# Half of one gate of an encoder block by seven products, in rows, with the sums of x kept on chip

## The chip, the cores and the metric

The kernel runs on one core of one Trainium2 chip, in one launch. The metric is the device time in microseconds (us). Five engines work side by side from queues of their own: TensorE (PE, matmuls; its weight loads are listed as PEld), VectorE (DVE), ScalarE (ACT), GpSimd (POOL) and SyncE (SP, which here only starts DMA transfers). SBUF is the working memory on the chip, with 128 partitions; PSUM holds the results of matmuls.

## The reference

One encoder block on x of 256 tokens by 2048 channels, in float32. What matters here is that eight pieces come out of one input projection, two branches are gated, and the result is merged:

```python
xn = rms_norm(x, norm_pre_w[l])
z = xn @ w_in[l]                       # 2048 x 13312
u_lru, g_lru, q, k, v, g_attn, m_lru, m_attn = jnp.split(z, split_at, axis=-1)
...
y_a = h.astype(x.dtype) * jax.nn.silu(g_lru)          # h: RG-LRU of the convolved u_lru, both directions
...
y_b = windowed_gqa(q, k, v, attn_sink[l]) * jax.nn.silu(g_attn)
merged = (jax.nn.sigmoid(m_lru) * (y_a @ w_proj_a[l])
          + jax.nn.sigmoid(m_attn) * (y_b @ w_proj_b[l]))
x = x + rms_norm(merged @ w_out[l], norm_post_w[l])
```

Each of g_lru, g_attn, m_lru and m_attn is 2048 columns wide. The change concerns the second 1024 columns of g_attn.

## The kernel before

**Numbers in two parts.** A product in float32 is made of products of a faster type, fp32r: each operand is split into a high part (a cast) and a low part (what the cast lost), and three products are added: high x high, high x low, low x high. A *half* of weights is a tile of 128 x 1024. ACT casts it to wh (`split`, L220), DVE subtracts to get wl (L222). The x parts, xs0 to xs7, are made once.

**Steps.** `load_plan` turns three written lists, START, MERGE and OUT, into steps; PE does them in that order. Each step uses 1 MB of weights, two halves. There are three kinds. A *blk* (letters g, h, w, k, q) is half of the sum for two column blocks of 128, so that "h8.0 h8.1" gives 256 columns of g_attn, with columns on partitions and the 256 tokens along the row (`add_pair`). A *quad* (u, v, p, b, o) is a quarter of 512 columns. A *part* (letters L, M, N, A, O: class `Seven`) belongs to a scheme that makes 1024 columns from seven products, m1 to m7, instead of eight, each of them in two parts (.0, .1); its results are in rows, tokens on partitions and columns along the row. The products need sums of blocks of x (`x_sums`) and sums of blocks of the weights. The weights' sums are built in *cells* of SBUF: a cell is loaded, and later blocks are added in flight by POOL's DMA (`accum_op`) or, for the pairs named in ADDED, by DVE (L225). The sums of x are made once, stored to DRAM as `away`, and loaded again for each part that needs them (`x_sum`, L357).

**What sets the order.** The program is written by the loop at the end of `body`, half by half. Transfers are issued 3 to 5 steps ahead (`fetch`), the cast four halves and the low part three halves ahead of PE (L1183 and on). Everything else is put at a tick of PE's order with `at` or `soon` (a part is one tick, other steps two): evacuations of PSUM, the chains of the RG-LRU (`lru_pair`, whose starts LRU shifts), attention heads (`heads`). Within an engine's queue the order is that of the program.

**Memory.** Most tiles of 4 KB a partition come from one pool of 45 *units* (`unit`); a new tile takes the place of the oldest one that is free, and waits for its last reader. PSUM has four single banks (`bank`) and two double ones (`banks`). Results that are needed much later are parked in DRAM: `park` stores a unit of 512 KB, `back` loads it.

**The gate that changes.** For "h", `silu_evac` copies the sums (ACT, L611), adds the low products (DVE, L604), scales by the row factor (DVE, L600), takes the sigmoid (ACT, L757) and multiplies (DVE, L758), then parks the unit `sga` when it has four blocks. For L, M, N and A, `gate_sum` combines the products (DVE, L784) and takes the sigmoid in rows (ACT, L792).

Of the kernel before, what the change touches and what calls it, by code (L numbers as in the profile page):

```python
# [21 lines left out]
P = 128  # L22
# [32 lines left out]


MERGE = """p0.0 p0.1 p0.2 p0.3 p1.0 p1.1 p1.2 p1.3 p2.0 p2.1 p2.2 Am1.0 p2.3 p3.0 p3.1 Am1.1 p3.2 Am5.0 p3.3
    b0.0 Am5.1 b0.1 Am3.0 b0.2 b0.3 Am3.1 b1.0 Am6.0 b1.1 b1.2 Am6.1 b1.3 Am7.0 b2.0 Am7.1 b2.1 Am2.0 b2.2 Am2.1 b2.3 Am4.0 b3.0
    Am4.1 Om1.0 b3.1 Om5.0 b3.2 b3.3""".split()
OUT = """o2.0 o2.1 Om1.1 o2.2 Om5.1 Om2.0 o2.3 Om3.0 Om6.0 Om3.1 o3.0 Om6.1 Om2.1 o3.1 Om7.0 Om7.1 Om4.0 Om4.1  # L60
    o3.2 o3.3""".split()

START = """u0.0 u0.1 u0.2 u0.3 v0.0 v0.1 v0.2 v0.3 g0.0 g0.1 h0.0 h0.1 w4.0 w4.1 g2.0 g2.1 h2.0 h2.1 w6.0 w6.1 g4.0 g4.1
    Lm1.0 h4.0 h4.1 Lm1.1 w8.0 Lm2.0 w8.1 Lm2.1 g6.0 Lm5.0 g6.1 h6.0 Lm5.1 h6.1 Lm3.0 w10.0 Lm3.1 w10.1 Lm6.0 g8.0
    Lm6.1 g8.1 h8.0 Lm7.0 h8.1 Lm7.1 w12.0 Lm4.0 w12.1 Lm4.1 g10.0 Mm1.0 g10.1 h10.0 Mm1.1 h10.1 Mm2.0 w14.0 Mm2.1
    w14.1 Mm5.0 g12.0 Mm5.1 g12.1 h12.0 Mm3.0 h12.1 Mm3.1 q0.0 Mm6.0 q0.1 Mm6.1 q0.2 q0.3 Mm7.0 g14.0 Mm7.1 g14.1
    Mm4.0 h14.0 Mm4.1 h14.1 Nm1.0 k0.0 k0.1 Nm1.1 k2.0 Nm2.0 k2.1 Nm2.1 q1.0 Nm5.0 q1.1 Nm5.1 q1.2 q1.3 Nm3.0 q2.0
    Nm3.1 q2.1 Nm6.0 q2.2 Nm6.1 q2.3 Nm7.0 q3.0 q3.1 Nm7.1 q3.2 Nm4.0 q3.3 Nm4.1""".split()
TURN = ((2, 6, 12, 15), (2, 6, 10, 13), (2, 6, 9, 11))
XSUM = (18, 22, 26, 30, 34, 38, 42, 46)  # L70
LRU = (-4, 0, 2, 2, 2, 2, 2, 4)
QUADS = {"u": ("w_in", U0), "v": ("w_in", V0), "p": ("w_proj_a", 0),
         "b": ("w_proj_b", 0), "o": ("w_out", 0)}
ADDED = {'A': {'m3': 'm6', 'm2': 'm4'}, 'O': {'m3': 'm6'}}
PAIRS = {"g": GL0, "h": GA0, "w": U0, "k": K0, "q": Q0}
SEVENS = {"L": ("w_in", ML0 + 1024), "M": ("w_in", ML0), "N": ("w_in", MA0), "A": ("w_in", MA0 + 1536), "O": ("w_out", 0)}


PV_CW = 0
# [37 lines left out]
def body(ctx, tc, x, x0, xT, wall, wlru, pvec, npost, ident_d, mask_d, rope_d, out):  # L117
# [9 lines left out]
    def unit(name, dt=F32, shape=(P, 4, S)):  # L127
        return units.tile(list(shape), dt, tag="u", name=name)
# [207 lines left out]
    def turned_sums_of(name, src, done):  # L336
# [9 lines left out]
        soon(lambda: parts_of(t[:, :, 0], t[:, :, 1], f))  # L346
        done(t)

    def x_sums(n):
        v = unit(f"xa{n}")  # L350
        nc.vector.tensor_tensor(v[:, 0:2], xs[n][:, :, 0].bitcast(F32), xs[n][:, :, 1].bitcast(F32), ALU.add)
        store = lambda t: nc.sync.dma_start(away[n // 4][:, :, n % 4], t.rearrange("p a b c -> p a (b c)").bitcast(F32))
        sums_of(f"xx{n}", v[:, 0:2], lambda t: soon(lambda: store(t), 7), v[:, 2:4])

    def x_sum(name, s, q):
        t = unit(name, F32R, (P, 4, 2, P))
# [3 lines left out]
    class Seven:  # L360
# [22 lines left out]
        def fetch(self, p, lead):  # L383
            m, q = p[2:]
            fresh = ("m1", "m3") if self.sums is None else ()
            if self.sums is None:
                if lead == 4 and m in fresh:
                    self.start(self.where(m), q)
                if lead == 4 and SEVEN[m][0][0] == "s":
                    self.kept[m, q] = x_sum(f"{self.name}{m}{q}", SEVEN[m][0], q)  # L390
            if lead == 5 and m in ("m5", "m6", "m7", "m4")[self.sums is not None:] and m not in ADDED.get(self.name, {}).values():
                load(self.cell(m, q), p, True)
# [356 lines left out]
    def silu_evac(units_list, n):  # L749
        def done(ps):  # L750
            if n % 4 == 0:
                units_list.append(unit(f"sg{n}"))
            dst = units_list[n // 4][:, n % 4:n % 4 + 2]

            def sigmoid():
                sg = half_unit(f"sig{n}", "p")
                nc.scalar.activation(sg, dst, AF.Sigmoid)  # L757
                soon(lambda: nc.vector.tensor_tensor(dst, dst, sg, ALU.mult))  # L758
# [27 lines left out]
    def gate_sum(gates, first=2, step=1):  # L786
# [177 lines left out]
    def heads(g, b, end):  # L964
        def start():
            h, l = unit(f"qh{g}", F32R), unit(f"ql{g}", F32R)
            parts_of(h, l, qs.pop(g))
            soon(lambda: back("sga", sga, g, (P, 4, S)), 6)
            for j in range(4):
                if j % 2 == 0:  # L970
                    both = {}
                head(4 * g + j, h, l, b + HEADS_AT[j], both, end)

        if g in QPARK:
            at(b - 8, lambda: back("q", qs, g, (P, 4, S)))
# [301 lines left out]
```

## Time and profile before

| | |
|---|---|
| median of 3 runs | 875.31 us (874.67 to 876.77) |
| profiled execution | 874.13 us |
| its span in the trace | 872.4 us |
| TensorE clock granted | 0.998 |
| PE, PEld busy | 99%, 85% |
| DVE, ACT, POOL busy | 84%, 74%, 7% |
| DMA | 248.96 MB, mean 285 GB/s |

In the rows of a profile, a group is "line engine operation out<-in shapes xcount | busy us, mean ns of one | idle time of the engine before them, and what ended it". A timeline row gives the start, the length and the work, with the idle time before it in brackets; neighbouring instructions of a group may overlap, so a price is taken from start to start. L12 is line 12 of the kernel. Tiles carry the names of the program: Lm1 is PSUM of product m1 of L, raw63 the weights of step 63, ga8 the PSUM of h8.

### The profile page before, as it was taken

The numbers are of one execution on the slowest core, as the hardware profiler recorded it, in microseconds if no ns is written. First come the engines' busy times: TensorE is split into PE (matmuls) and PEld (weight loads), VectorE is DVE, ScalarE is ACT, GpSimd is POOL, SyncE is SP. The second block draws the span as 40 slices with busy tenths as digits, with TensorE's granted clock in tenths as the row PEclk, the third lists the DMA queues.
The fourth block names the chain that finished last, engine by engine and source line by source line (L and its number), as shares of the span: only waits on it lengthen the run. The fifth ranks groups of instructions, "written<-read, shape, count | busy, mean of one in ns | idle before, by whom it ended". The sixth has DMA issues, their size and how long they took to land.

```text
span 872.4 us, 12283 instructions
## 1 busy us (share of the span) xinstructions
PE 862.8 (99%) x4450; PEld 739.7 (85%) x4450; DVE 736.4 (84%) x988; ACT 642.1 (74%) x923; POOL 62.5 (7%) x93
## 2 busy tenths in 40 slices
PE   9999999999999999999999999999999999999996
PEld 8888888888888888888888888888888888888885
DVE  6898999899797989789678688997669769999885
ACT  7689687878789696787776699976557455575654
POOL 0000001012000011100101100000000100000200
PEclk9999999999999999999999999999999999999999
DMA  8757599999959999996989996998999988988972
GB/s 322 288 195 231 204 358 250 351 335 285 330 212 270 311 296 319 300 324 219 299 326 305 301 323 204 311 315 329 301 293 365 305 302 244 327 296 319 257 196 97
DMA packets 66508, 248.96 MB, mean 285 GB/s; under 512 B 6416, under 2 KB 22544, under 8 KB 50960
## 3 DMA queue, kind: packets, MB, share of 16 engines
q1 hardware_dynamic: 52672, 208.86, 64.7%
q0 software_dynamic: 9792, 35.66, 21.1%
q10 hardware_dynamic: 3984, 3.67, 1.3%
q8 instruction: 35, 0.57, 0.3%
q14 instruction: 25, 0.20, 0.1%
HBM read 227.71 MB, written 20.45 MB: 284 GB/s over the span
## 4 chain that ended last, share of the span: by engine, by line
PE 88%; issue 4%; DVE 4%; DMA 2%; ACT 1%; SPq 0%; ACTq 0%; POOLq 0%; DVEq 0%
PE ga L256 7%; PE q L256 7%; PE gl L256 7%; PE u L256 5%; PE Mm L424 4%; PE Lm L424 4%; PE Nm L424 4%; PE ga L254 4%; PE gl L254 4%; PE q L254 4%; PE Om L424 3%; PE u L254 3%; PE pa__5770 L276 3%; PE pa__5514 L276 3%; PE o__7585 L276 3%
## 5 line engine op out<-in xcount | busy, mean ns | idle before, releaser
L222 DVE TENSOR_TENSOR wl<-raw,wh 128x1024 fp32r<-128x1024 f32 (+1 forms) x252 | 299.6, 1202 | 55.1 <-ACT wh L220 46.0
L220 ACT CAST wh<-raw 128x1024 fp32r<-128x1024 f32 (+1 forms) x251 | 253.8, 1035 | 67.2 <-DMA raw<-wall_dram 40.8
L256 PE MATMUL ga<-xs,wh 128*128 128x512 f32 x256 | 63.5, 391 | 0.0
L256 PE MATMUL gl<-xs,wh 128*128 128x512 f32 x256 | 63.4, 391 | 0.0
L256 PE MATMUL q<-xs,wh 128*128 128x512 f32 x256 | 63.2, 391 | 0.0
L256 PEld LDWEIGHTS gl<-xs,wh 128*128 128x128 f32 x256 | 47.0, 188 | 9.1
L256 PEld LDWEIGHTS q<-xs,wh 128*128 128x128 f32 x256 | 47.0, 188 | 9.0
L256 PEld LDWEIGHTS ga<-xs,wh 128*128 128x128 f32 x256 | 46.7, 188 | 8.8
L256 PE MATMUL u<-xs,wh 128*128 128x512 f32 x192 | 47.5, 391 | 0.0
L256 PEld LDWEIGHTS u<-xs,wh 128*128 128x128 f32 x192 | 35.2, 188 | 6.7
L254 PEld LDWEIGHTS q<-xs,wl 128*128 128x128 f32 x256 | 33.2, 191 | 1.2
L254 PEld LDWEIGHTS ga<-xs,wl 128*128 128x128 f32 x256 | 33.0, 191 | 1.2
L254 PE MATMUL q<-xs,wl 128*128 128x256 f32 x256 | 34.0, 283 | 0.0
L254 PEld LDWEIGHTS gl<-xs,wl 128*128 128x128 f32 x256 | 32.8, 191 | 1.2
L254 PE MATMUL ga<-xs,wl 128*128 128x256 f32 x256 | 33.5, 283 | 0.0
L254 PE MATMUL gl<-xs,wl 128*128 128x256 f32 x256 | 33.2, 283 | 0.0
L254 PEld LDWEIGHTS u<-xs,wl 128*128 128x128 f32 x192 | 24.6, 191 | 0.9
L254 PE MATMUL u<-xs,wl 128*128 128x256 f32 x192 | 24.9, 283 | 0.0
L673 DVE SCALAR_TENSOR_TENSOR uu<-upad,pv,uu 128x256 f32<-128x256 f32 x48 | 23.2, 483 | 1.7
L757 ACT ACTIVATE sig<-sg 128x512 f32<-128x512 f32 x16 | 10.2, 636 | 14.2 <-DVE sg L600 14.2
L896 DVE CUSTOM_DVE_ANT_0 p<-sc,table,pv 128x256 f32<-128x256 f32 x32 | 16.1, 540 | 5.1 <-PE sc L231 5.1
L902 ACT ACTIVATE p<-p,nm 128x256 f32<-128x256 f32 x32 | 16.0, 500 | 3.2 <-DVE nm L897 3.2
(519 smaller groups left out, 2085.6 us busy)
## 6 DMA issues: line engine op xcount, KB each, us to landing
raw<-wall_dram SPq DMA_DIRECT2D x121, 1024.0 KB, 7.7
lraw<-wlru_dram SPq DMA_DIRECT2D x8, 512.0 KB, 6.1
away<-xx SPq DMA_DIRECT2D x8, 512.0 KB, 8.7
Lm<-away SPq DMA_DIRECT2D x8, 512.0 KB, 12.6
Mm<-away SPq DMA_DIRECT2D x8, 512.0 KB, 13.8
Nm<-away SPq DMA_DIRECT2D x8, 512.0 KB, 14.6
turn<-pt SPq DMA_DIRECT2D x32, 128.0 KB, 5.0
pl<-turn SPq DMA_DIRECT2D x8, 512.0 KB, 7.2
```

Source lines behind the costliest of these rows:

```text
L220: cast(hs, raw)
L222: nc.vector.tensor_tensor(ls, raw, hs.bitcast(F32), ALU.subtract)
L254: nc.tensor.matmul(ps[:, 1], wl[:, sl], a[:, 0], start=False, stop=False)
L256: nc.tensor.matmul(ps, wh[:, sl], a, start=k == 0, stop=k == KT - 1)
L276: nc.tensor.matmul(got[t], a[:, i], (wl if low else wh)[:, sl], start=k + low + i == 0, stop=low == 1 and k == KT - 1)
L424: nc.tensor.matmul(self.ps[b], a[i], (wl if low else wh)[:, sl], start=fresh and j + low + i == 0, stop=last and j + low == 2, skip_group_ ...
L673: nc.vector.scalar_tensor_tensor(u, up[:, j, tap:tap + S], cw[:, tap:tap + 1], u, ALU.mult, ALU.add)
L757: nc.scalar.activation(sg, dst, AF.Sigmoid)
L896: nc.vector.tensor_tensor_reduce(p[:, t], sc[:, t], table["mask"][:, t], rtok_sc[:, t:t + 1], sk, ALU.add, ALU.max, m[:, t:t + 1])
L902: nc.scalar.activation(p[:, t], p[:, t], AF.Exp, bias=nm[:, t:t + 1], accum_out=dn[:, t:t + 1])
```

## The change

Eight steps, h8.0 to h14.1, go. A new Seven "H" gives the same 1024 columns in fourteen parts. Its results stand in rows, while the branch's attention output needs columns on partitions, so `silu_rows` does: combine (DVE), sigmoid with the tokens' scale (ACT, `hs`), scale and multiply (DVE), then a *turn*: four TensorE transposes into PSUM (`ht`), one copy by ACT into the same unit (`hr`), and a store of 256 KB by SP into `parksga`, so that four stores of 256 KB stand for two of 512 KB. A turn is put at the next start of the second step of a pair (`seconds`). The sums of x stay in SBUF from `x_sums` until M's m7; L, M and H read them there, and only N and A load them from `away`. N's m6 is built by DVE from m3's weights (ADDED) instead of by POOL. START is laid anew, mostly with two parts after a blk; in MERGE, Om1.0 and Om5.0 each move one step later; seven of the LRU's starts move to 0 or stay there; heads prepare one tick earlier.

```diff
-    b0.0 Am5.1 b0.1 Am3.0 b0.2 b0.3 Am3.1 b1.0 Am6.0 b1.1 b1.2 Am6.1 b1.3 Am7.0 b2.0 Am7.1 b2.1 Am2.0 b2.2 Am2.1 b2.3 Am4.0 b3.0
-    Am4.1 Om1.0 b3.1 Om5.0 b3.2 b3.3""".split()
+    b0.0 Am5.1 b0.1 Am3.0 b0.2 b0.3 Am3.1 b1.0 Am6.0 b1.1 b1.2 Am6.1 b1.3 Am7.0 b2.0 Am7.1 b2.1 Am2.0 b2.2 Am2.1 b2.3 Am4.0 b3.0 Am4.1 b3.1 Om1.0 b3.2 Om5.0 b3.3""".split()
...
-LRU = (-4, 0, 2, 2, 2, 2, 2, 4)
+LRU = (-4, 0, 0, 0, 0, 0, 0, 0)
...
-ADDED = {'A': {'m3': 'm6', 'm2': 'm4'}, 'O': {'m3': 'm6'}}
+ADDED = {'A': {'m3': 'm6', 'm2': 'm4'}, 'O': {'m3': 'm6'}, 'N': {'m3': 'm6'}}
...
-SEVENS = {"L": ("w_in", ML0 + 1024), "M": ("w_in", ML0), "N": ("w_in", MA0), "A": ("w_in", MA0 + 1536), "O": ("w_out", 0)}
+SEVENS = {"L": ("w_in", ML0 + 1024), "M": ("w_in", ML0), "N": ("w_in", MA0), "A": ("w_in", MA0 + 1536), "H": ("w_in", GA0 + 1024), "O": ("w_out", 0)}
...
+    seconds, hs, n = [], 0, 0
+    for p in plan:
+        if p[0] == "blk":
+            n += 1
+            if n % 2 == 0:
+                seconds.append(hs)
+        hs += 1 if p[0] == "part" else 2
...
-        sums_of(f"xx{n}", v[:, 0:2], lambda t: soon(lambda: store(t), 7), v[:, 2:4])
+        def done(t):
+            xsum[n] = t
+            soon(lambda: store(t), 7)
+
+        sums_of(f"xx{n}", v[:, 0:2], done, v[:, 2:4])
...
-                if lead == 4 and SEVEN[m][0][0] == "s":
+                if lead == 4 and SEVEN[m][0][0] == "s" and self.name in "NA":
...
+            elif self.name in "NA":
+                src = self.kept[m, q][:, j]
             elif self.sums is None:
-                src = self.kept[m, q][:, j]
+                src = xsum[n][:, SUMS.index(a)]
...
+                if self.name == "M":
+                    xsum.clear()
...
+    def silu_rows(g):
+
+        def done(t, c, ps, other, sign):
+            u = unit(f"hr{g}{c}{t}")
+            f, y = flat(u)[:, 0:512], u[:, 2:4].rearrange("p a (b s) -> p (a b) s", b=2)
+            rt = rtok[:, t:t + 1]
+
+            def sigmoid(src):
+                sg = flat(half_unit(f"hs{c}{t}", "p"))
+                nc.scalar.activation(sg, src, AF.Sigmoid, scale=rt)
+                soon(lambda: nc.vector.scalar_tensor_tensor(f, src, rt, sg, ALU.mult, ALU.mult))
+                at(min(b for b in seconds if b > now[0] + 2), turn)
+
+            def turn():
+                pt = banks(f"ht{c}{t}", (P, 4, P))
+                for j in range(4):
+                    nc.tensor.transpose(pt[:, j], f[:, j * P:(j + 1) * P], ident)
+                nc.scalar.copy(y, pt)
+                soon(store, 5)
+
+            def store():
+                key = "sga", g + c
+                if key not in parked:
+                    parked[key] = dram.tile([P, 1024], F32, name=f"parksga{g + c}")
+                nc.sync.dma_start(parked[key].rearrange("p (j s) -> p j s", j=4)[:, :, t * P:(t + 1) * P], y)
+
+            if other is None:
+                sigmoid(ps)
+            else:
+                combine(f, ps, other, sign)
+                soon(lambda: sigmoid(f))
+        return done
+
+    Seven("H", xs, None, silu_rows(2))
...
-        at(b - 2, start)
+        at(b - 3, start)
```

Three places of the order follow, each before and after. (In the changed kernel the lines of a helper stand some lower: the cast is L222, the low part L224.)

PE around the second pair of q0, in the middle of the first stage, before (q00 and q02 are the PSUM of q's two pairs, Mm1 that of a product of M, Mm61 the sums of x loaded for M's m6):

```order
L256 MATMUL q00_3579<-xs7_262,wh72_1_3603 128x512 x2
L424 MATMUL Mm1_2826<-wh73_0_3634,Mm61_3531 128x512 x4
L424 MATMUL Mm1_2826<-wl73_0_3635,Mm61_3531 128x512 x2
L424 MATMUL Mm1_2826<-wh73_1_3644,Mm61_3531 128x512 x4
L424 MATMUL Mm1_2826<-wl73_1_3645,Mm61_3531 128x512 x2
L256 MATMUL q02_3741<-xs0_123,wh74_0_3661 128x512 x2
L256 MATMUL q02_3741<-xs1_134,wh74_0_3661 128x512 x2
```

A part of M ends and the second pair of q0 begins. After, in the same pair, between its first and its second step:

```order
L435 MATMUL Mm1_3547<-wh74_1_3554,xs6_257 128x512 x2
L435 MATMUL Mm1_3547<-wh74_1_3554,xs7_262 128x512 x2
L435 MATMUL Mm1_3547<-wl74_1_3555,xs6_257 128x512
L435 MATMUL Mm1_3547<-wl74_1_3555,xs7_262 128x512
L831 MATMUL ht11_3645<-ident_92,hr211_3359 128x128 x4
L831 MATMUL ht01_3651<-ident_92,hr201_3540 128x128 x4
L258 MATMUL q02_3575<-xs0_123,wh75_0_3571 128x512 x2
```

M's part is now one of m1 and reads xs; behind it two turns, ht11 and ht01 (of the rows hr211 and hr201), stand next to each other.

ACT at the same place, before:

```order
L611 COPY q0f_3707<-q00_3579 128x512
L220 CAST wh75_0_3709<-raw75_3654 128x1024
L220 CAST wh75_1_3719<-raw75_3654 128x1024
L738 ACT_TABLE_LOAD
L738 ACTIVATE th12_3596<-th12_3596 128x1024
L436 COPY Mu_3735<-Mm1_2826 128x512
L220 CAST wh76_0_3737<-My0a_3251 128x1024
L853 COPY q0r_3758<-q0f_3707 32x256 x2
L220 CAST wh76_1_3763<-My0b_3252 128x1024
L792 ACT_TABLE_LOAD
L792 ACTIVATE mg1_3761<-mg1_3761,rtok_167 128x512
L220 CAST wh77_0_3786<-raw77_3729 128x1024
```

Casts of steps 75 to 77 with pieces of the LRU, of M and of q between them. After:

```order
L222 CAST wh75_0_3571<-raw75_3534 128x1024
L751 ACT_TABLE_LOAD
L751 ACTIVATE th12_3454<-th12_3454 128x1024
L222 CAST wh75_1_3597<-raw75_3534 128x1024
L222 CAST wh76_0_3623<-raw76_3564 128x1024
L222 CAST wh76_1_3633<-raw76_3564 128x1024
L832 COPY hr211_3359<-ht11_3645 128x512
L832 COPY hr201_3540<-ht01_3651 128x512
L447 COPY Mm1_3657<-Mm1_3547 128x512
L222 CAST wh77_0_3659<-raw77_3617 128x1024
```

The two copies of the turns stand behind the casts of steps 75 and 76, the second directly behind the first.

DVE around g12.0, which is step 63 in both orders, before (sg8_2583 is the unit of sga):

```order
L758 TENSOR_TENSOR sg8_2583<-sg8_2583,sig10_3119 128x512
L222 TENSOR_TENSOR wl61_1_3122<-raw61_3045,wh61_1_3121 128x1024
L222 TENSOR_TENSOR wl62_0_3151<-Mx0a_2663,wh62_0_3150 128x1024
L784 SCALAR_TENSOR_TENSOR mg0_3173<-Mm2_3068,Mm1_2995 128x512
L222 TENSOR_TENSOR wl62_1_3161<-Mx0b_2664,wh62_1_3160 128x1024
L222 TENSOR_TENSOR wl63_0_3176<-raw63_3141,wh63_0_3175 128x1024
L712 SCALAR_TENSOR_TENSOR th10_3114<-gr10_3019,th10_3114 128x1024
L222 TENSOR_TENSOR wl63_1_3202<-raw63_3141,wh63_1_3201 128x1024
L222 TENSOR_TENSOR wl64_0_3229<-Mx1a_2769,wh64_0_3228 128x1024
L604 TENSOR_TENSOR upad14_3224<-u14_3097,upad14_3224 128x2x256
```

The last work on h10 stands at the head. After:

```order
L224 TENSOR_TENSOR wl62_1_3048<-Hx0b_2353,wh62_1_3047 128x1024
L714 TENSOR_TENSOR gi10_2965<-gi10_2965,uu10_2762 128x512 x2
L224 TENSOR_TENSOR wl63_0_3073<-raw63_3029,wh63_0_3072 128x1024
L224 TENSOR_TENSOR wl63_1_3095<-raw63_3029,wh63_1_3094 128x1024
L224 TENSOR_TENSOR wl64_0_3126<-Hx1a_2439,wh64_0_3125 128x1024
L617 TENSOR_TENSOR upad14_3121<-u14_2945,upad14_3121 128x2x256
L613 TENSOR_TENSOR upad14_3121<-upad14_3121,rbc_93 128x2x256
L224 TENSOR_TENSOR wl64_1_3136<-Hx1b_2440,wh64_1_3135 128x1024
L735 TENSOR_TENSOR gr8_2553<-gr8_2553 128x512
L736 TENSOR_TENSOR sg8_2528<-gr8_2553,sg8_2528 128x512
```

That work is gone; wl62 and wl64, before of Mm5, are now of Hm6, and a sum and a product of the LRU have come here. The unit that wl63_1 takes is that of hr200, the first turned rows.

SP around the loads of steps 61 to 65, before:

```order
L208 DMA raw60_2976<-wall_dram 128x2048
L208 DMA raw61_3045<-wall_dram 128x2048
L357 DMA Mm50_3047<-away0_74 128x1024
L208 DMA raw63_3141<-wall_dram 128x2048
L357 DMA Mm51_3143<-away1_75 128x1024
L655 DMA lraw12_3198<-wlru_dram 128x1024
L208 DMA raw65_3221<-wall_dram 128x2048
```

Two loads of x sums for M's m5 stand between the raws. After:

```order
L210 DMA raw61_2922<-wall_dram 128x2048
L210 DMA raw63_3029<-wall_dram 128x2048
L668 DMA lraw12_3035<-wlru_dram 128x1024
L210 DMA raw65_3114<-wall_dram 128x2048
L839 DMA parksga2_3206<-hr200_2764 512x1x128
L210 DMA raw68_3231<-wall_dram 128x2048
```

They are gone, and the store of hr200 stands behind the load of raw65.

More of the change, by code (lines that the diff above doesn't have):

```diff
@@ L61 @@
     o3.2 o3.3""".split()
[L63 to L68, printed above, removed]
+START = """u0.0 u0.1 u0.2 u0.3 v0.0 v0.1 v0.2 v0.3 g0.0 g0.1 h0.0 h0.1 w4.0 w4.1 g2.0 g2.1 h2.0 h2.1 w6.0 w6.1 g4.0 g4.1 h4.0 h4.1 Lm1.0 w8.0 Lm1.1 Lm2.0 w8.1 Lm2.1 g6.0 Lm5.0 g6.1 Lm5.1 h6.0 Lm3.0 Lm3.1 h6.1 Lm6.0 Lm6.1 w10.0 Lm7.0 w10.1 Lm7.1 g8.0 Lm4.0 Lm4.1 g8.1 Hm1.0 w12.0 Hm1.1 w12.1 Hm2.0 Hm2.1 g10.0 Hm5.0 g10.1 Hm5.1 w14.0 Hm3.0 Hm3.1 w14.1 Hm6.0 g12.0 Hm6.1 g12.1 Hm7.0 Hm7.1 q0.0 Hm4.0 q0.1 Hm4.1 Mm1.0 q0.2 Mm1.1 q0.3 Mm2.0 g14.0 Mm2.1 Mm5.0 g14.1 Mm5.1 k0.0 Mm3.0 Mm3.1 k0.1 Mm6.0 k2.0 Mm6.1 k2.1 Mm7.0 Mm7.1 q1.0 Mm4.0 q1.1 Mm4.1 q1.2 Nm1.0 Nm1.1 q1.3 Nm2.0 q2.0 Nm2.1 q2.1 Nm5.0 Nm5.1 q2.2 Nm3.0 q2.3 Nm3.1 Nm6.0 q3.0 Nm6.1 q3.1 Nm7.0 q3.2 Nm7.1 q3.3 Nm4.0 Nm4.1""".split()
@@ L347, in turned_sums_of @@
         done(t)
+    xsum = {}
     def x_sums(n):
@@ L643, in body @@
         at(DECAY + i // 2, fn)
-    sgl, sga = [], []
+    sgl, sga = [None] * 4, [None] * 4
     ya, yb = [None] * 8, [None] * 8
@@ L751, in done @@
             if n % 4 == 0:
-                units_list.append(unit(f"sg{n}"))
+                units_list[n // 4] = unit(f"sg{n}")
             dst = units_list[n // 4][:, n % 4:n % 4 + 2]
```

## The prediction

> **What bounds the kernel now.** I read the page first, then the waits of PE and of its weight loads, then the windows of the stage that is rewritten. The page's busy times:
>
> ```profile
> PE 862.8 (99%) x4450; PEld 739.7 (85%) x4450; DVE 736.4 (84%) x988; ACT 642.1 (74%) x923; POOL 62.5 (7%) x93
> ```
>
> PE is busy for 862.8 of 872.4 us. That alone could be flattered by modelled ends, so the waits come next. Columns: who waited for whom, us in total, times, longest.
>
> ```profile
> PEld u_ps L568 <- ACT wh L220: 1.2, 3, 0.6
> PEld Om L424 <- DVE wl L222: 0.7, 2, 0.5
> PE u_ps L568 <- ACT wh L220: 0.4, 1, 0.4
> ```
>
> Only the opening (u_ps) and one place late in the program (Om) have PE waiting for data at all. The windows (PE, PEld, DVE, ACT, POOL busy; granted clock; DMA share; GB/s) say the same of the first stage:
>
> ```profile
> 100.00:150.00 50.00, 50.00 (x298) 44.59 (x297) 49.20 (x70) 39.97 (x58) 3.23 (x4) 1.00 0.89 293
> 150.00:200.00 50.00, 50.00 (x278) 43.69 (x278) 45.36 (x54) 40.62 (x56) 5.91 (x11) 1.00 1.01 331
> 200.00:250.00 50.00, 50.00 (x278) 43.73 (x277) 42.82 (x50) 39.69 (x54) 5.35 (x8) 1.00 0.94 289
> 300.00:350.00 50.00, 50.00 (x278) 43.69 (x278) 43.19 (x50) 41.19 (x55) 6.96 (x8) 1.00 0.98 315
> ```
>
> PE is gapless at full clock, even where DVE is busy 49.20 of 50 us and where the DMA engines are full. So PE's work taken away here is time gained one for one, as long as DVE, ACT and the units of SBUF keep up; they have no time to win, only time to lose.
>
> **The change on PE.** One Lm part and one block that follows it, in PE's timeline (start, length, work):
>
> ```profile
> 160.48 1.07 PE L424 MATMUL Lm<-wh,xs 128*128 128x512 f32 x4
> 161.39 0.61 PE L424 MATMUL Lm<-wl,xs 128*128 128x512 f32 x2
> 161.84 1.07 PE L424 MATMUL Lm<-wh,xs 128*128 128x512 f32 x4
> 162.75 0.61 PE L424 MATMUL Lm<-wl,xs 128*128 128x512 f32 x2
> 163.20 1.98 PE L256 MATMUL u<-xs,wh 128*128 128x512 f32 x8
> 165.01 2.08 PE L254 MATMUL u<-xs,wl 128*128 128x256 f32 x16
> 166.93 2.00 PE L256 MATMUL u<-xs,wh 128*128 128x512 f32 x8
> 168.77 1.07 PE L424 MATMUL Lm<-wh,xs 128*128 128x512 f32 x4
> ```
>
> Start to start, a part is 163.20 - 160.48 = 2.72 us and a block 168.77 - 163.20 = 5.57 us. Eight blocks of the gate go: 8 x 5.57 = 44.56 us. Fourteen parts of "H" come: 14 x 2.72 = 38.08 us. Four turns of four transposes come. The kernel before has the same form of turn once, near its end:
>
> ```profile
> 789.65 0.71 PE L1029 MATMUL mt<-ident,mg 128*128 128x128 f32 x4
> 790.12 1.17 PE L276 MATMUL o__7585<-wh,ms 128*128 128x512 f32 x4
> 790.40 0.59 ACT L149 CAST ms<-mt 128x512 fp32r<-128x512 f32 x1 [5.10 <-PE mt L1029]
> ```
>
> From the first transpose to the next matmul is 790.12 - 789.65 = 0.47 us, so four turns are 1.88 us. PE's sum: -44.56 + 38.08 + 1.88 = -4.60 us.
>
> On this price the Trainium skill differs: "TensorE: Matmul & The Clock Gate", Part 4, gives about 275 ns for a 128 x 128 bf16 transpose within a kernel. If sixteen stood one behind the other, an estimate from that page is 4.4 us instead of 1.88, and PE's sum would be -2.1. The row above, four in 0.47 us, decides for overlap.
>
> The second gain is in MERGE. There the weights' low halves come late (idle before in brackets):
>
> ```profile
> 765.56 0.30 PEld L424 LDWEIGHTS Om<-wl,ms 128*128 128x128 f32 x2 [0.21 <-DVE wl L222]
> 767.30 0.30 PEld L424 LDWEIGHTS Om<-wl,ms 128*128 128x128 f32 x2 [0.51 <-DVE wl L222]
> ```
>
> Two parts stood in a row there (Am4.1, Om1.0), and after one piece of pb the next, Om5.0. With a piece of pb ahead of each, DVE has more time per half. The waits are 0.72 us together, of which PE's own pipeline already hides some; the gain is between 0 and 0.7, and I take 0.3. The ceiling of the change is then -4.60 - 0.3 = -4.9 us.
>
> **What it costs the other engines.** Groups of before, mean ns of one in the last column but the idle time:
>
> ```profile
> L222 DVE TENSOR_TENSOR wl<-raw,wh 128x1024 fp32r<-128x1024 f32 x244 | 294.1, 1219 | 53.1 <-ACT wh L220 44.0 <-PE Mm L424 3.3 <-DMA turnm<-mt 3.2
> L220 ACT CAST wh<-raw 128x1024 fp32r<-128x1024 f32 x244 | 249.5, 1047 | 65.4 <-DMA raw<-wall_dram 39.2 <-PE Am L424 8.5 <-PE pa__6021 L276 5.5
> L225 DVE TENSOR_TENSOR Ax0a<-Ax0a,raw 128x1024 f32<-128x1024 f32 x1 | 1.2, 1220 | 0.0
> L784 DVE SCALAR_TENSOR_TENSOR mg<-Mm,Mu 128x512 f32<-128x512 f32 x1 | 0.7, 691 | 0.8 <-ACT Mu L436 0.8
> L600 DVE TENSOR_TENSOR sg<-sg,rbc 128x512 f32<-128x512 f32 x16 | 11.1, 692 | 0.6
> L604 DVE TENSOR_TENSOR sg<-ga,sg 128x512 f32<-128x512 f32 x8 | 5.5, 685 | 1.2 <-ACT sg L611 1.2
> L758 DVE TENSOR_TENSOR sg<-sg,sig 128x512 f32<-128x512 f32 x16 | 10.9, 683 | 0.0
> L757 ACT ACTIVATE sig<-sg 128x512 f32<-128x512 f32 x16 | 10.2, 636 | 14.2 <-DVE sg L600 14.2
> L611 ACT COPY sg<-ga 128x512 f32<-128x512 f32 x8 | 4.7, 588 | 12.8 <-PE ga L256 12.8
> ```
>
> A part has two halves of weights as a block has, so 28 halves come and 16 go: 12 more. DVE: 12 x 1.219 = 14.6; four sums for N's m6 (the L225 form) 4 x 1.22 = 4.9; the old evacuation 4 x (0.685 + 0.692 + 0.683) = 8.2 goes; three combines and four products of the L784 form, 7 x 0.69 = 4.8, come. In all +16.1 us. ACT: 12 x 1.047 = 12.6; 4 x (0.588 + 0.636) = 4.9 goes; four sigmoids and seven copies, 4 x 0.636 + 7 x 0.588 = 6.7, come. In all +14.4 us. Averaged, DVE goes from 736 to 752 of some 870 us, ACT from 642 to 656: both still run beside PE. If that cover were gone, DVE's 16.1 would be paid; this is the second rival. DMA gets less: sixteen x sums of 512 KB no longer come back (8 MB), N's m6 drops 2 MB, H's parts add 6 MB of weights. PE does not wait for a load in the rows above, so I take nothing for it, neither gain nor loss.
>
> **The new waits.** (a) Two turns, ht11 and ht01, fall on the same tick inside q0, one right behind the other, into the same PSUM buffer: ht01 waits until ACT has copied ht11 out. By the row at 789.65, ACT begins 790.40 - 789.65 = 0.75 us after the first transpose and copies for 0.59; I add 0.1 for the way back to PE, an estimate from the 0.04 us between 790.36, where the transposes end, and ACT's start. PE would have gone on after 0.47, so the wait is 0.75 + 0.59 + 0.1 - 0.47 = 1.0 us, if ACT is free. On ACT the copy stands behind casts three halves ahead of PE. At the like place of before:
>
> ```profile
> 352.04 1.05 ACT L220 CAST wh<-Mx0b 128x1024 fp32r<-128x1024 f32 x1
> 354.60 1.98 PE L256 MATMUL q<-xs,wh 128*128 128x512 f32 x8
> ```
>
> PE starts q0's first block at 354.60; the cast three halves ahead ended at 353.09, 1.5 us before. So ACT is in time unless it lags 1.5 us more. Bounds 1.0 and 3; I take 1.0, because the margin covers the lag.
>
> (b) The units. x sums stay in SBUF (8 of 45 units), and H's cells and rows come on top. Counted in allocation order, all 45 units are taken around H's and M's middle; before, at most 39 ahead of the tail. Then a new tile waits for the last reader of an old one. The one that matters is wl63_1 (g12.0): its unit is that of hr200, the first turned rows, so DVE waits for hr200's store to land. The landings (KB each, median us):
>
> ```profile
> raw<-wall_dram SPq DMA_DIRECT2D x121, 1024.0 KB, 7.7
> away<-xx SPq DMA_DIRECT2D x8, 512.0 KB, 8.7
> turn<-pt SPq DMA_DIRECT2D x32, 128.0 KB, 5.0
> parksga<-sg SPq DMA_DIRECT2D x4, 512.0 KB, 11.6
> ```
>
> From the turn's start t: copy done at t + 1.4, store issued about t + 1.7. The LRU's taps and two splits in a row on DVE:
>
> ```profile
> L673 DVE SCALAR_TENSOR_TENSOR uu<-upad,pv,uu 128x256 f32<-128x256 f32 x48 | 23.2, 483 | 1.7
> 766.03 2.36 DVE L222 TENSOR_TENSOR wl<-raw,wh 128x1024 fp32r<-128x1024 f32 x2
> ```
>
> From wl63_1 to wl65_1 DVE has five splits and an LRU scaling of that size (6 x 1.22), four pieces of 0.69 and six taps of 0.483, 13.0 us; neighbours overlap a little (2.36 for two splits, not 2.44), so I take 12.4. PE reads wl65_1 after the turn (0.47), the blocks w14.1 and g12.0 (11.14), two H parts (5.44) and half a block (2.75), at t + 19.8. DVE must therefore go on by t + 7.4; it does so at t + 1.7 + L. The store has 256 KB: a third of the way from turn's 128 KB (5.0) to 512 KB (8.7, the shorter of the two) gives L = 6.2, so it is 0.5 us late. Bounds 0 (L = 5.0) and 5.9 (L = 11.6); I keep to the low side because the nearer row in size is turn's. (c) The other tiles that wait for a unit wait for readers some 3 to 4 us of PE's work back, at least 5 before: 0 to 2, taken at 0.3, since the halves are split at least three ahead.
>
> Sum: -4.9 + 1.0 + 0.5 + 0.3 = -3.1 us. From the profiled execution, 874.13 (872.4 of span), to 871.0; the median of three runs stands 1.18 above, so 875.31 - 3.1 = 872.2 us.
>
> **Rivals.** 1. None of the waits is paid: another engine's lead covers them. -4.9, 870.4 us. For it: PE rode over 98% of DVE. Against: (a) is a chain on one buffer that nothing hides.
>
> 2. DVE becomes the bound. The new order has mostly two parts to a block. Before, a part and a block take 8.29 us of PE and 4 x 1.219 = 4.88 of DVE's splits, 29.4 per 50 us; the window at 150 shows 45.36, so other work is 15.9. With two parts and a block, 11.01 us, the splits are 7.31, or 33.2 per 50 us; with 15.9 that is 49.1. On the mean it just fits, as 49.20 did; where the LRU chains bunch, it doesn't. Half a microsecond short per 50 us over some 250 us is 2.5, and with the waits -4.9 + 1.8 + 2.5 = -0.6: 874.7 us (873.5 to 876). By the window at 200 (42.82) there are 2.5 us more to spare, which speaks against it.
>
> 3. Slower: hr200's store lands like parksga, on full DMA queues (share 1.01 at 150). DVE stops at wl63_1, and PE runs out of low halves 5.9 us: -4.9 + 1.0 + 5.9 + 0.3 = +2.3, 877.6 us; each microsecond of landing beyond 11.6 adds one, so at L = 13 it is 879.0. The point from which it decides is L = 9.3, where the gain is gone; by over 0.3% it is slower from L = 11.9. For it: the four parksga stores. Against: half the size.
>
> The same page of the Trainium skill (Part 1 and "HAM oscillation") says that idle gaps of PE above about 3.4 us halve its clock for a while. No row of before shows this, the clock is 1.00 throughout; it could add to rival 3 alone.
>
> 4. Transposes pay their full time. The tile's row (count; min, median, max in ns):
>
> ```profile
> L1029 PE MATMUL mt<-ident,mg x8: 270/272/329, 789.7 to 793.3; 128*128 128x128 f32 x8
> ```
>
> Sixteen of 0.272 are 4.35 us, 2.5 more than taken: -0.6, 874.7 us. The start of the next matmul 0.47 us after four speaks against it.
>
> **How the numbers follow.** About 0.3%, 2.6 us, is what a measurement of this kernel can tell from no change. The forecast has 0.42, rival 1 0.17, rival 2 0.27, rival 3 0.12, rival 4 0.02. The forecast's own spread (waits of 1 to 4) is 871.4 to 874.4; 0.31 of its 0.42 lies below 872.7. Faster: 0.17 + 0.31 = 0.48. Slower: 0.11 of rival 3 (beyond 877.9, or beside some of rival 2) and 0.02 of rival 2's far end, 0.13. Same: the rest, 0.39. The range from 870.0 to 877.0 takes in the forecast, rivals 1, 2 and 4, and leaves out rival 3 and a little of rival 1's far side, 0.16.
>
> **What would show it.** Right: matmuls of Hm at 2.72 us a part; one wait of about 1 us of PE at ht on ACT's copy (L832); DVE waiting under a microsecond for the store at the wl of g12; no wait of Om on wl at the end of MERGE. Wrong: PE waiting for wl (L224) through the two-part stretches with DVE busy at 49 or more of 50 (rival 2); one wait of several us at g12 on parksga2's landing (rival 3); no waits at all (rival 1); a turn of more than 0.6 us to the next matmul where no wait is shown (rival 4).

## The result, and the profile after

The changed kernel takes 885.44 us (884.68 to 887.5) against 875.31 before: the ratio is 1.012, with a 95% interval of 1.011 to 1.0131. It is 10.1 us slower, where 3.1 us faster were forecast. Its profiled execution took 884.68 us, of which 882.9 are the span. The page after:

```profile
PE 862.4 (98%) x4378; PEld 733.9 (83%) x4378; DVE 750.3 (85%) x999; ACT 657.3 (74%) x939; POOL 73.0 (8%) x105
```

DVE has 13.9 us more work than before and ACT 15.2 more, near the 16.1 and 14.4 that were worked out. The waits of PE are another list than before:

```profile
PE gl L256 <- DVE wl L224: 5.1, 2, 3.9
PE o L232 <- DVE pl L144: 1.8, 2, 1.3
PE ht L831 <- ACT hr L832: 1.7, 1, 1.7
PE spin L479 <- POOL eps L481: 1.0, 1, 1.0
PE u_ps L581 <- ACT wh L222: 0.9, 1, 0.9
PE Mm L435 <- DVE wl L224: 0.7, 1, 0.7
PE pb__7010 L278 <- DVE wl L224: 0.6, 1, 0.6
PE gate L231 <- ACT gi L710: 0.5, 1, 0.5
```

The largest has this history in the timeline (start, length, work; idle time before it and what ended it in brackets):

```profile
302.44 0.60 PE L831 MATMUL ht<-ident,hr 128*128 128x128 f32 x4
303.08 0.59 ACT L832 COPY hr<-ht 128x512 f32<-128x512 f32 x1
303.69 0.52 SPq L839 DMA_DIRECT2D parksga<-hr  x1
316.77 1.23 DVE L224 TENSOR_TENSOR wl<-raw,wh 128x1024 fp32r<-128x1024 f32 x1 [10.02 <-DMA parksga<-hr]
318.05 1.41 PE L256 MATMUL gl<-xs,wl 128*128 128x256 f32 x8 [3.92 <-DVE wl L224]
329.33 1.22 PE L256 MATMUL gl<-xs,wl 128*128 128x256 f32 x8 [1.15 <-DVE wl L224]
```

The turn of hr200 is at 302.44 and its store is started at 303.69. DVE then stands still for 10.02 us at wl63_1, whose unit that store still reads, and goes on at 316.77: the store took 13.0 us to land, the longest transfer of parksga's tile in this kernel. PE runs out of low halves for 3.92 us, and again for 1.15. In short windows around it (PE, PEld, DVE, ACT, POOL busy; granted clock; DMA share; GB/s):

```profile
310.00:314.00 4.00, 4.00 (x23) 3.38 (x21) 0.00 (x0) 3.97 (x7) 0.00 (x0) 1.00 1.06 214
314.00:318.00 4.00, 0.13 (x2) 0.00 (x0) 1.23 (x2) 3.26 (x4) 0.00 (x0) 1.00 0.95 332
318.00:319.20 1.20, 1.15 (x8) 1.15 (x9) 1.20 (x2) 0.00 (x0) 0.00 (x0) 0.88 0.79 123
319.20:322.20 3.00, 3.00 (x9) 2.38 (x8) 2.96 (x4) 0.00 (x0) 1.08 (x2) 0.50 0.83 304
```

DVE does nothing from 310 to 314, PE next to nothing from 314 to 318, and from 319.2 to 322.2 the granted clock is 0.50. Two more stores hold somebody up, parkya0 (started at 180.05) and parkq0 (at 392.88):

```profile
194.52 0.47 ACT L709 ACTIVATE gr<-gate,pv 128x256 f32<-128x256 f32 x1 [5.09 <-DMA parkya<-sg]
410.98 1.23 DVE L224 TENSOR_TENSOR wl<-My1a,wh 128x1024 fp32r<-128x1024 f32 x1 [5.62 <-DMA parkq<-q0f]
412.26 0.72 PE L435 MATMUL Mm<-wl,xx 128*128 128x512 f32 x2 [0.73 <-DVE wl L224]
```

They land 14.4 and 18.0 us after their start. And the two turns in a row:

```profile
367.45 2.92 ACT L222 CAST wh<-raw 128x1024 fp32r<-128x1024 f32 x3
368.63 0.60 PE L831 MATMUL ht<-ident,hr 128*128 128x128 f32 x4
370.27 0.57 ACT L832 COPY hr<-ht 128x512 f32<-128x512 f32 x1
370.90 0.66 PE L831 MATMUL ht<-ident,hr 128*128 128x128 f32 x4 [1.67 <-ACT hr L832]
371.31 1.40 PE L258 MATMUL q<-xs,wh 128*128 128x512 f32 x5
```

ACT comes to the first copy only when three casts are done, and the second turn waits 1.67 us for it.

To see what all of it is worth I took every matmul's time to the start of the next and subtracted 227 ns (128x512) or 119.5 ns (128x256), what they take undisturbed. What is left over, the surplus, is 5.6 us in the kernel before, 2.6 of it ahead of 50 us, and 19.4 us after. The new surplus lies mainly at four kinds of places: the stores, 9.3 us (0.9 at 194, 6.9 at 314 to 330 with 1.4 of it in the stretch of the slower clock, 1.5 at 411 to 414); the two turns in a row, 1.7 at 369 (counted apart, transposes are not in the 19.4); the heads, 3.6 at 558 to 580; MERGE, 0.5 more than before, at 751 and 777. With PE's own -4.6 these places make +10.5; the span grew by 10.5. (That they meet to the tenth is chance: some 0.4 of new surplus lies elsewhere, and the -4.6 is a forecast.)

### The profile page after: what moved, and what is told of

It is laid out like the page before. It is cut to its first block, busy times and chain, and to the rows that moved or that the text cites. A ratio compares the mean times of both kernels' runs of the same rounds, so it can differ in the third digit from the quotient of the medians.

```text
span 882.9 us, 12249 instructions
## 1 busy us (share of the span) xinstructions
PE 862.4 (98%) x4378; PEld 733.9 (83%) x4378; DVE 750.3 (85%) x999; ACT 657.3 (74%) x939; POOL 73.0 (8%) x105
## 4 chain that ended last, share of the span: by engine, by line
PE 81%; DMA 5%; DVE 5%; issue 4%; ACT 2%; SPq 1%; ACTq 1%; POOLq 0%; DVEq 0%
PE q L258 6%; PE gl L258 6%; PE u L258 5%; PE Lm L435 4%; PE Nm L435 4%; PE Hm L435 4%; PE Am L435 3%; PE ga L258 3%; PE q L256 3%; PE gl L256 3%; PE Om L435 3%; PE Mm L435 3%; PE pb__7297 L278 2%; PE pa__5741 L278 2%; PE pa__5992 L278 2%
## 5 line engine op out<-in xcount | busy, mean ns | idle before, releaser
L224 DVE TENSOR_TENSOR wl<-raw,wh 128x1024 fp32r<-128x1024 f32 (+1 forms) x240 | 285.2, 1201 | 53.1 <-ACT wh L222 38.6
L222 ACT CAST wh<-raw 128x1024 fp32r<-128x1024 f32 (+1 forms) x239 | 241.1, 1035 | 60.9 <-DMA raw<-wall_dram 31.1
L258 PE MATMUL ga<-xs,wh 128*128 128x512 f32 x128 | 31.8, 391 | 0.0
L258 PEld LDWEIGHTS ga<-xs,wh 128*128 128x128 f32 x128 | 23.3, 189 | 4.3
L709 ACT ACTIVATE gr<-gate,pv 128x256 f32<-128x256 f32 x32 | 15.2, 475 | 5.9 <-DMA parkya<-sg 5.1
L231 PE MATMUL gate<-ul,lwh 128*128 128x256 f32 x64 | 18.2, 284 | 0.5 <-ACT gi L710 0.5
L233 PE MATMUL gate<-ul,lwl 128*128 128x256 f32 x64 | 18.1, 283 | 0.0
```

The source lines that it names most:

```text
L222: cast(hs, raw)
L224: nc.vector.tensor_tensor(ls, raw, hs.bitcast(F32), ALU.subtract)
L231: nc.tensor.matmul(ps, wh, xh, start=start, stop=False, skip_group_check=more)
L233: nc.tensor.matmul(ps, wl, xh, start=False, stop=stop, skip_group_check=more)
L258: nc.tensor.matmul(ps, wh[:, sl], a, start=k == 0, stop=k == KT - 1)
L709: nc.scalar.activation(v["gr"][:, 2 * d + j], ps[:, 0], AF.Sigmoid, bias=pv[:, PV_BR + b:PV_BR + b + 1])
```

## The experiments

**The sums of x loaded again** (x1).

```diff
-                if lead == 4 and SEVEN[m][0][0] == "s" and self.name in "NA":
+                if lead == 4 and SEVEN[m][0][0] == "s":
...
-            xsum[n] = t
```

> The changed kernel, but with the sums of x loaded again from DRAM for L, M and H as well, so that they don't hold 8 units. Theory (the full pool makes DVE and ACT wait for stores to land: the waits of PE at 194, 314 to 330 and 393 to 414 us, 0.9 + 6.9 + 1.5 = 9.3 us): those three are gone, the time falls by 8 to 9.5 us to about 876.5, with the turn's wait (1.7) and those of 550 to 580 us (3.6) left. Rival (DVE has too little time in the stretches with two parts to a block, the stores only happen to be named): most of the waits stay as waits on wl without a DMA behind them, less than 3 us gained. Rival (the 12 MB of loads that come back fill SP's queue): waits of ACT for raw grow, and the gain is under 5 us.

892.65 us, ratio 1.0204 (1.0188 to 1.022): 7 us slower than the changed kernel. The waits on stores are there still, at other tiles, and ACT waits for raws 51.3 us instead of 31.1:

```profile
DVE wl L224 <- DMA parkya<-sg: 8.1, 1, 8.1
ACT wh L222 <- DMA raw<-wall_dram: 51.3, 29, 4.7
ACT wh L222 <- DMA parkq<-q0f: 3.1, 1, 3.1
ACT Hu L444 <- DMA parksga<-hr: 2.2, 1, 2.2
```

Loaded sums take units too, one per part from four steps ahead; by a count of the program's order 38 to 41 units of 45 are in use where it was 45, and a unit still comes round before its store has landed. The theory's forecast failed here, the second rival (the queue of loads) had a share in it; the edit was no clean test of either.

**The turn of hr201 a pair later** (x2).

```diff
-            rt = rtok[:, t:t + 1]
+            rt, late = rtok[:, t:t + 1], 4 if (t, c) == (1, 0) else 0
...
-                at(min(b for b in seconds if b > now[0] + 2), turn)
+                at(min(b for b in seconds if b > now[0] + 2 + late), turn)
```

> The changed kernel, but the turn of hr201 a pair later (in g14.1), so that two turns no longer stand next to each other. Theory (the second turn waits for ACT's copy out of the same PSUM buffer): the wait of 1.7 us at the turns is gone, 883.7. Rival (ACT is that late by itself, and the turn only the first to meet it): PE waits as long for a wh or a copy a little later, 885.4 as after.

892.11, ratio 1.0184 (1.0163 to 1.0205): 6.7 us slower. The turn's wait is gone, but ACT's cast of step 84 now gets the unit of parkq0's tile, and PE loses 5.2 us at Mm, one wait of 4.6:

```profile
ACT wh L222 <- DMA parkq<-q0f: 6.5, 1, 6.5
PE Mm L435 <- DVE wl L224: 5.2, 2, 4.6
```

So a small move of the order can re-deal which tile gets which unit, and with it which store is waited for.

**Stores on ACT's queue** (x3): in `park` and in `store` of `silu_rows`, `nc.sync.dma_start` becomes `nc.scalar.dma_start`.

> The changed kernel, but the stores of the parked units and of the turned rows started by ACT's queue instead of SP's. Theory A (a store lands late since it stands behind the loads of raw in SP's queue): landings fall from 13 to 18 us to 3 to 7, and the waits at 194, 314 and 411 us go: 8 to 9 us gained, about 877. Theory B (the sixteen DMA engines are full whatever the queue): landings stay over 10 us, and the time is within 2 us of 885.4.

881.57, ratio 1.0075 (1.0062 to 1.0088): 3.9 us of the expected 8 gained. The turned rows' stores land after 5.1 us in the median, 9.1 on SP:

```profile
parksga<-hr ACTq DMA_DIRECT2D x4, 256.0 KB, 5.1
```

and PE's waits at 314 and 411 are gone. But an early landing is not what ended the one at 314:

```profile
308.76 1.23 DVE L224 TENSOR_TENSOR wl<-raw,wh 128x1024 fp32r<-128x1024 f32 x1 [0.17 <-PE u L256]
318.42 0.62 ACTq L839 DMA_DIRECT2D parksga<-hr  x1
329.96 0.69 DVE L797 SCALAR_TENSOR_TENSOR hr<-Hm,Hu 128x512 f32<-128x512 f32 x1 [2.43 <-DMA parksga<-hr]
```

In ACT's queue the store of hr200 stands behind ACT's own work. It starts only at 318.42 and lands 11.4 us later, after the time at which it landed from SP's queue. wl63_1, the row at 308.76, does not wait for it, so it must have got another unit; a combine of H's rows waits in its place, 2.43 us. How much of the 3.9 us comes from shorter landings and how much from units dealt otherwise is not separated. The turns' wait grows to 2.7, and MERGE loses 2.9 us at two places.

**Both of these together** (y1), and with q3.3 between the last two parts of START (y3: `Nm7.1 Nm4.0 q3.3 Nm4.1`).

> Stores of parked units and turned rows on ACT's queue, and the turn of hr201 one pair later (the two edits that ran alone before, together). Theory (once stores land early the later turn costs nothing, and its wait of 2.85 us in the run with ACT's queue goes): 881.6 - 2.5 = about 879. Rival (the stores' landing still decides which wait comes; the later turn moves a unit under another wait, as it did alone): no gain, 881 to 884.

> The same, and at the end of START q3.3 between Nm4.0 and Nm4.1 instead of ahead of both. Theory (ACT is crowded at 550 to 580 us because the last two parts stand in a row behind q3, beside the heads' casts): the waits of PE there, 2.4 us, shrink by 1 to 2. Rival (the heads' casts crowd it whatever the order): the same time as the run without this edit.

892.19, ratio 1.02 (1.0181 to 1.0219), and 897.62, ratio 1.0264 (1.0247 to 1.0282). In both, hr201's store, now behind parkq0's in ACT's queue, is the one that is waited for:

```profile
ACT wh L222 <- DMA parksga<-hr: 12.6, 1, 12.6
PE k L258 <- ACT wh L222: 8.6, 1, 8.6
```

The transfers of parksga's tile in y1:

```profile
DMA to landing us min/median/max: 3.4/7.7/23.6
```

The store was started at 401.4, ACT goes on at 425.0 and PE at 426.1, so the longest is this one. ACT's queue is no cure: there too a store can take 23.6 us. In y3 the end of START gets its own wait, N's last part for DVE's combine (4.4 us), so that edit was worse than what it was to mend.

**Heads prepared two ticks ahead as before** (x4: `at(b - 2, start)`).

> The changed kernel, but heads prepared two ticks ahead of their start, as before, instead of three. Theory (the earlier casts of q crowd ACT at 550 to 580 us): the waits of PE there, 3.6 us, go, about 882. Rival (ACT is crowded there by the end of START, two Nm parts in a row with the evacuation of q3 and the y parts, whatever the tick): they stay, 885.4 or a little more.

885.57, ratio 1.0119 (1.0103 to 1.0134): no change. In its trace (an execution of 892.12, so not a typical one) the waits stand at 547 and 584 on ql instead of 558 to 580 on pl. The third tick alone isn't the cause; the rival holds as far as it goes.

**The kept sums alone, in the kernel before** (y2), and **the kernel before with `UNITS = 40`** (b_u40).

> The kernel before with one part of the change alone: the sums of x stay in SBUF until M's m7, L and M read them there, and their sixteen loads go. The order and PE's work are those of before. Theory (the pool of units: with 8 more taken, up to 45 of 45 are in use at 190 to 230 and 340 to 370 us, and the units of parkya0, parksga or parkya1, and parkya2 are taken again within 4 us of PE's work, while their stores take 10 to 14): waits of ACT on these stores, PE waits that before does not have, 2 to 8 us slower, 877.5 to 883. Rival (the new order, with two parts to a block, makes the waits): within 1 us of 875.4, or faster by the loads that are gone.

> The kernel before with 40 units instead of 45, nothing else. Theory (free units decide): in the first stage the units of parkya0, parkya1 or parksga and parkya2 come round after about 5 us of PE's work instead of 8 to 10, and ACT or DVE waits for their stores; waits at the heads too (530 to 660 us), where units come round after 1 to 8; 3 to 12 us slower. Rival (units never bind): within 1 us of 875.4.

876.63, ratio 1.0016 (1.0004 to 1.0028), and 895.0, ratio 1.0228 (1.0215 to 1.0241). With the pool filled to 45, ACT does wait for two stores in the order of before, but PE does not feel it:

```profile
ACT wh L220 <- DMA parkya<-sg: 4.8, 1, 4.8
ACT wh L220 <- DMA parksga<-sg: 2.7, 1, 2.7
```

So in the order of before, a full pool and waits of 3 to 5 us for a store come with a loss of no more than 1.5 us. That this is because a block stands behind each part there is likely, but not shown. With five units fewer the same kernel loses 20 us; in its trace (an execution of 899.07, 4 us above the median) 5.7 us are lost at 225 to 275 us, and most of the rest at the heads and in MERGE. Few free units do make this kernel slow.

**Stores that hold no unit** (w1).

```diff
-                nc.sync.dma_start(parked[key].rearrange("p (j s) -> p j s", j=4)[:, :, t * P:(t + 1) * P], y)
+                nc.sync.dma_start(parked[key].rearrange("p (j s) -> p j s", j=4)[:, :, t * P:(t + 1) * P], xs[2 * c + t][:, :, :, 0:P].rearrange("p a b s -> p (a b) s").bitcast(F32))
...
-        nc.sync.dma_start(d, flat(t))
+        nc.sync.dma_start(d, xs[c].rearrange("p a b c -> p (a b c)").bitcast(F32))
```

This kernel leaves out that the results are parked: parts of x are stored and loaded back in their place, so it times the transfers but does not compute the block. The same holds for w2 and w4.

> The changed kernel, but every store of a parked unit and of turned rows reads a tile of x's parts (xs), which is never taken again in that time, instead of the result; bytes, rows, queue and order of the transfers stay. So no unit waits for a store to land (the parked values are not the result's). Theory (units held by stores that land late, in an order that gives DVE and ACT little lead, make most of the loss): the waits at 194, 314 to 330 and 393 to 414 us go, 9.3 us in all, 885.4 - 9 = 876.5; what is left are the turns (1.7), the stretch of 550 to 580 us (3.6) and MERGE. Rival (DVE is short in the two-part stretches, and the waits only come up elsewhere): under 4 us gained, with waits on wl behind ACT's casts in their place.

875.74, ratio 1.0012 (1.0001 to 1.0023): 9.7 us less than the changed kernel, where 9 were expected. Same transfers, same order in the queue, a pool of the same size; the stores read other tiles. With that a store need not wait for ACT's copy either: the one of hr200 starts some 5 us earlier, at 298.83. It takes 17.9 us to land, and nothing waits for it. The windows of its first stage, against 44.92 of PE at 300 to 350 in the changed kernel:

```profile
300.00:350.00 50.00, 50.00 (x274) 43.44 (x273) 46.10 (x55) 45.73 (x65) 5.67 (x9) 1.00 0.85 259
400.00:450.00 50.00, 50.00 (x259) 42.74 (x258) 41.75 (x47) 41.02 (x54) 5.23 (x6) 1.00 0.95 288
```

PE is gapless there with DVE at 46.10 of 50. That settles it between the two: what the stores held up made the loss, not a lack of DVE's time. That it was the units, and not the later start of the stores, is shown by v1 below.

**The turn of hr201 in a single bank of PSUM**, with free stores (w2) and alone (w3).

```diff
-                pt = banks(f"ht{c}{t}", (P, 4, P))
+                pt = (bank if (c, t) == (0, 1) else banks)(f"ht{c}{t}", (P, 4, P))
```

> The same, and the turn of hr201 into one of the single banks of PSUM, at its place, so that it has not to wait for ACT's copy of the turn ahead. Theory: the wait of 1.7 us is gone too, 1.5 us below the run without this edit, about 875. Rival (ACT is late there, and the next thing that needs ACT waits instead; or the single bank is waited for): no gain.

> The changed kernel with the turn of hr201 into a single bank of PSUM, nothing else. Theory: 1.7 us less, 883.7, with the waits on stores as they were. Rival (as with the turn a pair later, which cost 6.7 us: any move of ACT's or PE's time there changes which unit a store holds up): 885 to 892.

876.57, ratio 1.0013 (1.0003 to 1.0024), and 884.53, ratio 1.0107 (1.009 to 1.0125). The turn's wait is gone in both traces. With free stores nothing is gained, since two waits on wl of 0.9 and 1.0 us come at 382 and 386 in its place; alone the gain of 0.9 us is within the interval. With free stores the rival was right: DVE and ACT were late there anyway, and the turn only met it first. Alone, the run lies between theory and rival.

**The heads two ticks later** (`HEAD0 = -14`), with free stores and the single bank (w4), in the changed kernel alone (v2), and in the kernel before (v3).

> The run with free stores and the single bank, and the heads two ticks later (HEAD0 -14 instead of -16). Theory (ACT is crowded at 550 to 580 us by the heads' casts meeting the end of N): the waits there, 2.4 to 3.6 us, shrink, 872 to 874. Rival (the crowd is N's end and the y parts; later heads only have less lead in MERGE): the same or 1 to 3 us slower.

> The changed kernel with the heads two ticks later, nothing else. Theory (what the heads cost at 550 to 580 us is a term of its own, 3.6 us and some of MERGE, beside the stores'): 881 to 882.5. Rival (it helped only where the stores were free): within 1 us of 885.4.

> The kernel before with the heads two ticks later, nothing else. Theory (the crowd at the heads comes with the new end of START and the heads' earlier preparation; before has no waits of PE there): within 1 us of 875. Rival (later heads are better whatever the order): 2 us or more faster than before.

871.55, ratio 0.9957 (0.9943 to 0.9971); 881.67, ratio 1.0077 (1.0054 to 1.0101); 876.5, ratio 1.0012 (1.0003 to 1.002). Later heads gain 5.0 us beside w2, 3.8 alone, and lose 1.4 in the kernel before. The windows of that stretch, of the kernel before, of the changed one and of w4:

```profile
535.00:585.00 50.00, 50.00 (x248) 42.36 (x248) 46.73 (x89) 47.32 (x86) 0.00 (x0) 1.00 0.86 295
```

```profile
540.00:590.00 50.00, 47.78 (x229) 39.06 (x228) 45.76 (x83) 47.95 (x86) 0.00 (x0) 1.00 0.79 276
```

```profile
540.00:590.00 50.00, 50.00 (x238) 41.84 (x237) 45.38 (x87) 43.94 (x81) 0.00 (x0) 1.00 0.84 289
```

ACT was busy 47.32 of 50 us before, without a wait of PE, and 47.95 in the changed kernel, with 2.22 us of idle PE; with the heads later it is 43.94 and PE gapless. So the crowd on ACT is a term of its own that came with the new order. Which part of the new order brought it is open: the third tick alone did not (x4), and y3's edit at the end of START made it worse. In the kernel before, neither theory nor rival is met: later heads are not better there, but 1.4 us worse.

**A full kernel that gives units out later** (v1): the changed one, with the single bank, HEAD0 -14, and

```diff
+    held = const.tile([P, 1], F32, name="held")
+
+    def hold(t):
+        if now[0] < HOLD:
+            soon(lambda: nc.vector.tensor_copy(held, flat(t)[:, 0:1]), 6)
...
         nc.sync.dma_start(d, flat(t))
+        hold(t)
```

and the same for the turned rows (`hold(u)`; HOLD is tick 230, the first stage). DVE's read of one column is the last reader of the unit, so the pool gives it out only after that.

> A full kernel: the changed one, in which DVE reads one column of each parked or turned unit of the first stage six ticks after its store is started, so that the unit is given out again only then; with hr201's turn in a single bank and the heads two ticks later. Theory (it is the store's landing on a unit that is given out too soon which costs the 9 us; six ticks, some 15 us, cover the landings of 13 to 18): near the run with free stores, 872 to 874, faster than before. Rival (the units held longer are missing elsewhere: the pool is full, and other tiles wait for PE's readers): 876 to 884.

873.11, ratio 0.9971 (0.996 to 0.9982): 2.0 us faster than the kernel before, 12.3 faster than the changed one. Of these 12.3, later heads were worth 3.8 alone (v2) and the single bank 0.9 at most (w3), which leaves about 7.6 for the later units. Its waits of PE:

```profile
PE gl L257 <- DVE wl L225: 1.2, 2, 0.8
PE spin L480 <- POOL eps L482: 1.0, 1, 1.0
PE u_ps L582 <- ACT wh L223: 0.6, 1, 0.6
PE gate L232 <- ACT gi L711: 0.6, 1, 0.6
PE Mm L436 <- DVE wl L225: 0.4, 1, 0.4
```

No store of the first stage is waited for. The store of hr200 itself is as it was, 13.1 us to its landing (the last row here, from the list of DMA issues: KB, us to landing), and wl63_1 goes ahead of it:

```profile
303.52 0.53 SPq L840 DMA_DIRECT2D parksga<-hr  x1
306.74 1.23 DVE L225 TENSOR_TENSOR wl<-raw,wh 128x1024 fp32r<-128x1024 f32 x1 [0.17 <-PE u L257]
parksga<-hr SPq DMA_DIRECT2D x1, 256.0 KB, 13.1
```

So it was the unit that cost the time, not the transfer. The surplus at 375 to 400 is 2.6 us; whether other tiles wait for units there is not shown.

## Why the prediction was wrong

**The sum on PE held.** The turn's transposes, four in 0.47 us, came as priced (from the row at 370.90 to the next matmul it is 0.41, from that at 302.44 it is 0.36), so rival 4 is out. One behind the other, the Trainium skill's 275 ns ("TensorE: Matmul & The Clock Gate", Part 4) would be 1.1 us, which these rows don't show either. With the waits taken away the work saved shows as time in part, 3.2 us below before in w4 and 2.0 in v1.

**Step (b) failed by its size.** The mechanism was named with its tile: wl63_1 waits for the store of hr200. But the landing L was taken at 6.2 us, from turn's 128 KB and the shorter of the 512 KB rows, kept "to the low side"; it was 13.0, beyond the 11.6 that stood as the end of the range. By the prediction's own formula, 1.7 + 13.0 - 7.4 = 7.3 us late, and 6.9 were lost where 0.5 stood in the sum. The rest of the step held: DVE's work from wl63_1 to wl65_1, taken at 12.4 us, ran from 316.77 to 329.3. That is rival 3's mechanism at rival 3's price, which got 0.12; but with L = 13 rival 3 gives 879 us, and the other 6 us are the terms below. The mistake was to take a median for one transfer, where the profile before had this row for the transfers of parksga's tile:

```profile
DMA to landing us min/median/max: 6.0/8.2/20.4
```

The longest of them is a store, of 512 KB, started at 215.5. What decides is this store in this stretch, and the bound had to be the longest.

**Step (c) failed too.** The units that wait were said to wait for PE's readers, 0.3 us. Two of them waited for stores as well, parkya0's and parkq0's, 2.4 us of surplus.

**The clock** was put aside as something that could add to rival 3. It did fall: behind 3.92 us of idle PE it was 0.50 for some 3 us. This agrees with what the Trainium skill says ("TensorE: Matmul & The Clock Gate", "HAM oscillation") of gaps above about 3.4 us; the waits of 1.67 us at the turn and of 1.15 had no such tail. That it cost time of its own is not shown: DVE worked on without a wait, busy 12.28 of the 12.56 us from 316.77 to 329.33, and PE's next wait ended with it. At full clock PE would by this have waited longer there, instead of 1.15 us.

**Step (a)** was 1.7 instead of 1.0: ACT's copy began 1.64 us after the first transpose, not 0.75, behind three casts (the margin of 1.5 us at the like place did not hold). As a term it was worth little: w2 shows that without it others wait instead.

**The heads were not looked at.** Preparing them a tick earlier and the new end of START were put at nothing, without a reason. ACT, busy 47.32 of 50 us there before, had little room; 3.6 us were lost in the trace, and later heads won back 3.8 to 5.0. The earlier tick alone was not it (x4).

**MERGE** did not give 0.3; the wait of Om is gone, but pb waits for wl at 751, 0.5 us more in all.

**Rival 2** (DVE as the bound) is refuted as a main cause by w1: PE is gapless at 300 to 350 with DVE at 46.10 of 50.

What stays open: why a store of 256 KB lands after 5 us once and after 13 to 24 another time. The queue alone doesn't decide it (x3 against y1).

## What to carry to other kernels

A store holds its tile until it lands; in a pool with few free tiles the oldest free one is the next given out, so look up, for every store, how long after it its tile comes round, and compare that with the longest landing in the trace, not the median. If it's too short, keep the tile from being given out (a late reader of one column does) rather than hurry the store. And when steps get shorter, the same number of steps of lead is less time, so a wait that cost nothing before may stop the bound engine (y2 against the changed kernel points that way; no run here isolates it).

## What the runs showed of the hardware

Landings of stores from SBUF to DRAM vary widely. 256 KB from SP's queue took 9.1 us in the median and 13.0 at most in the changed kernel; from ACT's queue it took 5.1 in the median and 11.4 at most in x3, and 23.6 in y1. 512 KB took up to 18.0 in the changed kernel and 20.4 in the kernel before. While the store of 13.0 us was on its way, the DMA engines' share was 1.06 at 310 to 314 us and 0.95 at 314 to 318.

After a stop of PE of 3.92 us the granted clock was 0.88 on the mean of the next 1.2 us and 0.50 in the 3 us behind them. After stops of 1.67 and 1.15 us it stayed at 1.00.
